# Batch norm with ReLU on one core: the read of `beta` moves from the scalar queue to the gpsimd queue

## The chip, the cores and the metric

The kernel runs on one core of a Trainium2 chip. The metric is the device time in microseconds (us) of one execution. The kernel before took 83.83 us, the median of 4 runs between 83.75 and 84.23 us. A core has five engines, each with its own instruction stream: TensorE (PE), VectorE (DVE), ScalarE (ACT), GpSimd (POOL) and SyncE (SP). Data moves between HBM and on-chip memory by DMA: an engine issues a transfer from its stream (the profile writes SPq, ACTq, POOLq for that), and 16 DMA engines, shared by all queues, carry it out in packets.

## The reference, cut to what matters

The input `x` is [32, 128, 32, 32] in float32, so 16.78 MB; the output has the same size. Four vectors of 128 numbers hold the parameters of each channel.

```python
def reference(x, gamma, beta, running_mean, running_var, eps):
    normalized = (x - running_mean[None, :, None, None]) / np.sqrt(running_var[None, :, None, None] + eps)
    scaled = normalized * gamma[None, :, None, None] + beta[None, :, None, None]
    return np.maximum(scaled, 0).astype(np.float32)
```

Per channel this is one multiply, one add and a ReLU: `relu(x * scale + bias)` with `scale = gamma / sqrt(running_var + eps)` and `bias = beta - running_mean * scale`.

## The kernel before

**Tiling.** Batch and channel are flattened into 4096 rows of 1024 numbers (4 KB). A partition takes J = 16 rows that lie next to each other, so 128 partitions hold 2048 rows, and there are two such halves (t = 0 and 1). `PIECES` cuts each half along the 16 rows: rows 0-2, 2-4, 4-8 and 8-16 of half 0, rows 0-8 and 8-16 of half 1. That makes six load tiles of 1, 1, 2, 4, 4 and 4 MB (in units of 1024 KB). Each has its own buffer, so no load waits for a buffer.

**Loads.** All six are issued on the sync queue (line 52), in that order. Each partition of a tile is one packet, of 8, 8, 16, 32, 32 and 32 KB.

**Parameters.** Because 16 rows are 16 neighbouring channels, a partition needs 16 channels, and partitions 0 to 7 together need all 128; the pattern repeats every 8 partitions. The four vectors are read into the tile `raw`, 8 partitions by 4 by 16, by four transfers of 512 bytes on the scalar queue (line 59), in the order running_var, gamma, running_mean, beta. GpSimd makes a 0/1 matrix `rep` meanwhile (lines 63 and 64), and one matmul (line 74) of `rep` with `raw` spreads the four vectors to 128 partitions (`cols`). The matmul reads the whole of `raw`, so it waits for all four transfers. Then follow a square root on ScalarE (line 82, with a load of its function table before it) and four small operations on VectorE (lines 84 to 90), which end in `scale_t` and `bias_t`.

**Main loop.** ScalarE goes over the tiles in load order; one activation (line 96) does one row of all partitions, 128 x 1024, in place, and at the end of a tile the same queue issues its store (line 104). `STORE_CUTS` has the first tile stored in two parts of 512 KB, so there are seven stores. ScalarE's order is the program's own (`manual_schedule`); on the other engines the framework orders the instructions.

**Semaphores.** Each transfer counts up a semaphore when it has landed. In the trace of the kernel before, the seventeen transfers of the two queues share eight of these in turn. A transfer that takes a semaphore over waits, on the issuing queue, until the one that had it before has landed: the fourth load waits for running_var, the fifth for running_mean, the sixth for the second load.

**End.** After the last store has landed, SyncE checks the semaphores in turn, all engines meet at a barrier, and GpSimd clears the semaphores (line 138).

Of the kernel before, what the change touches and what calls it, by code (L numbers as in the profile page):

```python
# [1 line left out]

# [4 lines left out]


F32 = mybir.dt.float32
ACTF = mybir.ActivationFunctionType  # L10

J = 16

PIECES = (((0, 2), (2, 4), (4, 8), (8, 16)), ((0, 8), (8, 16)))

STORE_CUTS = {(0, 1)}


@with_exitstack
def kernel(
    ctx: ExitStack,
    tc: tile.TileContext,
    x: bass.AP,
    gamma: bass.AP,
    beta: bass.AP,
    running_mean: bass.AP,
    running_var: bass.AP,
    eps: bass.AP,  # L30
    out: bass.AP,
):
    nc = tc.nc
    B, C, H, W = x.shape
    HW = H * W
    P = nc.NUM_PARTITIONS
    assert C % J == 0 and P % (C // J) == 0 and (B * C) % (P * J) == 0
    Q = C // J
    T = B * C // (P * J)

    xr = x.rearrange("b c h w -> (b c) (h w)").rearrange("(t p j) w -> t p j w", p=P, j=J)
    outr = out.rearrange("b c h w -> (b c) (h w)").rearrange("(t p j) w -> t p j w", p=P, j=J)

    data = ctx.enter_context(tc.tile_pool(name="data", bufs=1))
    params = ctx.enter_context(tc.tile_pool(name="params", bufs=1))
    psum = ctx.enter_context(tc.tile_pool(name="psum", bufs=1, space=bass.MemoryType.PSUM))

    tiles = []
    for t in range(T):
        for a, b in PIECES[t]:  # L50
            xt = data.tile([P, b - a, HW], F32, name=f"x{t}_{a}")
            nc.sync.dma_start(out=xt, in_=xr[t, :, a:b, :])  # L52
            tiles.append((t, a, b, xt))

    raw = params.tile([Q, 4, J], F32, name="raw")
    for k, src in enumerate((running_var, gamma, running_mean, beta)):
        nc.scalar.dma_start(out=raw[:, k, :], in_=src.rearrange("(q j) -> q j", j=J))
    eps_t = params.tile([P, 1], F32, name="eps_t")  # L60
    nc.vector.memset(eps_t, float(eps))  # L61
    rep = params.tile([Q, P // Q, Q], F32, name="rep")
    nc.gpsimd.memset(rep, 1.0)  # L63
    nc.gpsimd.affine_select(  # L64
        out=rep,
        in_=rep,
        compare_op=mybir.AluOpType.is_equal,
        fill=0.0,
        base=0,
        pattern=[[0, P // Q], [-1, Q]],  # L70
        channel_multiplier=1,
    )
    cols = psum.tile([P, 4, J], F32, name="cols")
    nc.tensor.matmul(  # L74
        cols.rearrange("p k j -> p (k j)"),
        rep.rearrange("q r s -> q (r s)"),
        raw.rearrange("q k j -> q (k j)"),
        start=True,
        stop=True,
    )  # L80
    std_t = params.tile([P, J], F32, name="std_t")
    nc.scalar.activation(out=std_t, in_=cols[:, 0, :], func=ACTF.Sqrt, bias=eps_t[:, 0:1], scale=1.0)  # L82
    rstd_t = params.tile([P, J], F32, name="rstd_t")
    nc.vector.reciprocal(out=rstd_t, in_=std_t)  # L84
    scale_t = params.tile([P, J], F32, name="scale_t")
    nc.vector.tensor_mul(out=scale_t, in0=cols[:, 1, :], in1=rstd_t)  # L86
    ms_t = params.tile([P, J], F32, name="ms_t")
    nc.vector.tensor_mul(out=ms_t, in0=cols[:, 2, :], in1=scale_t)  # L88
    bias_t = params.tile([P, J], F32, name="bias_t")
    nc.vector.tensor_sub(out=bias_t, in0=cols[:, 3, :], in1=ms_t)  # L90

    with tc.manual_schedule(engines={mybir.EngineType.Activation}):
        for t, a, b, xt in tiles:
            first = a
            for j in range(a, b):
                nc.scalar.activation(  # L96
                    out=xt[:, j - a, :],
                    in_=xt[:, j - a, :],
                    func=ACTF.Relu,
                    bias=bias_t[:, j : j + 1],  # L100
                    scale=scale_t[:, j : j + 1],
                )
                if j + 1 == b or (t, j + 1) in STORE_CUTS:
                    nc.scalar.dma_start(
                        out=outr[t, :, first : j + 1, :], in_=xt[:, first - a : j + 1 - a, :]
                    )
                    first = j + 1


# [1 line left out]
_INS = ['x', 'gamma', 'beta', 'running_mean', 'running_var', 'eps']  # L111
_OUTS = [((32, 128, 32, 32), 'float32')]

_NUMBERS = {'eps': 1e-05}


# [26 lines left out]
```

## Time and profile before

| What | Where from | Value |
|---|---|---|
| Time of the profiled execution | times | 83.75 us |
| Its span, first to last instruction | profile page | 81.9 us |
| Median of the runs | times | 83.83 us |
| ScalarE busy | page, part 1 | 38.5 us (47%) |
| GpSimd busy | page, part 1 | 0.8 us (1%), all of it before 1.5 us |
| HBM traffic | page, part 3 | 16.78 MB read, 16.78 MB written |
| Issue of the four parameter reads on ACT | timeline | 0.59, 0.29, 0.31 and 0.39 us, from 0.81 to 2.48 us |
| Start of the matmul that needs them | timeline | 7.49 us |
| First activation of the main loop | timeline | 9.48 us |
| Last store issued | timeline | 55.93 us |

The span is what the profiler sees of the program's own instructions; 1.85 us of the execution's time lie outside it. The issue of a transfer (an ACTq or SPq line) is only the time in which the engine's queue hands it over. The transfer itself runs afterwards on the DMA engines, and whoever needs the data shows up with a wait "<-DMA ...". Idle time before an instruction stands in square brackets behind it in a timeline, with what ended it.

### The profile page before, as it was taken

The numbers are of one execution on the slowest core, as the hardware profiler recorded it, in microseconds if no ns is written. First come the engines' busy times: TensorE is split into PE (matmuls) and PEld (weight loads), VectorE is DVE, ScalarE is ACT, GpSimd is POOL, SyncE is SP. The second block draws the span as 40 slices with busy tenths as digits, with TensorE's granted clock in tenths as the row PEclk, the third lists the DMA queues.
The fourth block names the chain that finished last, engine by engine and source line by source line (L and its number), as shares of the span: only waits on it lengthen the run. The fifth ranks groups of instructions, "written<-read, shape, count | busy, mean of one in ns | idle before, by whom it ended". The sixth has DMA issues, their size and how long they took to land.

```text
span 81.9 us, 119 instructions
## 1 busy us (share of the span) xinstructions
PE 0.7 (1%) x2; PEld 0.5 (1%) x2; DVE 0.8 (1%) x5; ACT 38.5 (47%) x34; POOL 0.8 (1%) x6
## 2 busy tenths in 40 slices
PE   0003000000000000000000000000000000000000
PEld 0002000000000000000000000000000000000000
DVE  0000300000000000000000000000000000000000
ACT  0600477799039999199994199993000000000000
POOL 3000000000000000000000000000000000000000
DMA  1999998989899999979799798998999799699690
GB/s 36 352 405 481 416 520 352 512 352 496 368 464 400 460 404 460 436 308 588 320 396 564 328 440 384 512 512 352 416 512 432 336 512 480 288 512 496 272 512 0
DMA packets 1936, 33.56 MB, mean 410 GB/s; under 512 B 272, under 2 KB 272, under 8 KB 528
## 3 DMA queue, kind: packets, MB, share of 16 engines
q1 hardware_dynamic: 864, 16.78, 48.4%
q10 hardware_dynamic: 1072, 16.78, 47.8%
HBM read 16.78 MB, written 16.78 MB: 410 GB/s over the span
## 4 chain that ended last, share of the span: by engine, by line
DMA 56%; ACT 11%; SPq 0%; issue 0%
DMA x<-in_x_dram 56%; ACT x L96 11%; SPq L52 0%
## 5 line engine op out<-in xcount | busy, mean ns | idle before, releaser
L96 ACT ACTIVATE x<-x,bias_t,scale_t 128x1024 f32<-128x1024 f32 x32 | 37.0, 1227 | 10.5 <-DMA x<-in_x_dram 8.1
L82 ACT ACT_TABLE_LOAD x1 | 1.3, 1283 | 2.6 <-issue 2.6
L82 ACT ACTIVATE std_t<-cols,eps_t 128x16 f32<-128x16 f32 x1 | 0.3, 274 | 4.3 <-PE cols L74 4.3
L74 PE MATMUL cols<-raw,rep 8*128 8x64 f32 x2 | 0.7, 428 | 7.5 <-DMA raw<-in_beta_dram 7.5
L74 PEld LDWEIGHTS cols<-raw,rep 8*128 8x128 f32 x2 | 0.5, 306 | 7.5 <-issue 7.5
L64 POOL TENSOR_SCALAR_AFFINE_SELECT rep<-rep 8x128 f32<-8x128 f32 x1 | 0.4, 393 | 0.1
L84 DVE RECIPROCAL rstd_t<-std_t 128x16 f32<-128x16 f32 x1 | 0.3, 255 | 7.5 <-ACT std_t L82 7.5
L63 POOL MEMSET rep<- 8x128 f32 x1 | 0.2, 194 | 0.3 <-POOLq L124 0.3
L86 DVE TENSOR_TENSOR scale_t<-cols,rstd_t 128x16 f32<-128x16 f32 x1 | 0.2, 174 | 0.1
L88 DVE TENSOR_TENSOR ms_t<-cols,scale_t 128x16 f32<-128x16 f32 x1 | 0.2, 174 | 0.0
L90 DVE TENSOR_TENSOR bias_t<-cols,ms_t 128x16 f32<-128x16 f32 x1 | 0.2, 174 | 0.0
L124 POOL MEMSET const-bfloat16-1.0<- 128x1 bf16 x1 | 0.1, 108 | 0.0
L124 POOL MEMSET const-uint8-127<- 128x1 uint8 x1 | 0.1, 108 | 0.0
L124 POOL MEMSET const-float32-0.0<- 128x1 f32 x1 | 0.1, 105 | 0.3 <-issue 0.3
L124 POOL MEMSET const-float32-1.0<- 128x1 f32 x1 | 0.1, 105 | 0.0
L61 DVE MEMSET eps_t<- 128x1 f32 x1 | 0.1, 59 | 0.9 <-PEq L124 0.9
## 6 DMA issues: line engine op xcount, KB each, us to landing
x<-in_x_dram SPq DMA_DIRECT2D x3, 4096.0 KB, 38.7
out_dram<-x ACTq DMA_DIRECT2D x3, 4096.0 KB, 28.0
x<-in_x_dram SPq DMA_DIRECT2D x2, 1024.0 KB, 5.7
x<-in_x_dram SPq DMA_DIRECT2D x1, 2048.0 KB, 11.2
out_dram<-x ACTq DMA_DIRECT2D x1, 2048.0 KB
out_dram<-x ACTq DMA_DIRECT2D x2, 512.0 KB, 19.0
out_dram<-x ACTq DMA_DIRECT2D x1, 1024.0 KB
raw<-in_running_var_dram ACTq DMA_DIRECT2D x1, 0.5 KB
```

Of the source, the lines that this page charges most:

```text
L61: nc.vector.memset(eps_t, float(eps))
L63: nc.gpsimd.memset(rep, 1.0)
L64: nc.gpsimd.affine_select(out=rep, in_=rep, compare_op=mybir.AluOpType.is_equal, fill=0.0, base=0, pattern=[[0, P // Q], [-1, Q]], channel ...
L74: nc.tensor.matmul(cols.rearrange("p k j -> p (k j)"), rep.rearrange("q r s -> q (r s)"), raw.rearrange("q k j -> q (k j)"), start=True, s ...
L82: nc.scalar.activation(out=std_t, in_=cols[:, 0, :], func=ACTF.Sqrt, bias=eps_t[:, 0:1], scale=1.0)
L84: nc.vector.reciprocal(out=rstd_t, in_=std_t)
L86: nc.vector.tensor_mul(out=scale_t, in0=cols[:, 1, :], in1=rstd_t)
L88: nc.vector.tensor_mul(out=ms_t, in0=cols[:, 2, :], in1=scale_t)
L90: nc.vector.tensor_sub(out=bias_t, in0=cols[:, 3, :], in1=ms_t)
L96: nc.scalar.activation(out=xt[:, j - a, :], in_=xt[:, j - a, :], func=ACTF.Relu, bias=bias_t[:, j : j + 1], scale=scale_t[:, j : j + 1],)
L124: nc = _bacc.Bacc("TRN2", target_bir_lowering=False, num_devices=1)
```

## The change

The loop over the four vectors chooses the queue by the source: `beta` is issued by gpsimd, the other three by scalar as before. Source, destination and size of each transfer are as before, and so is everything else in the program text.

```diff
     raw = params.tile([Q, 4, J], F32, name="raw")
     for k, src in enumerate((running_var, gamma, running_mean, beta)):
-        nc.scalar.dma_start(out=raw[:, k, :], in_=src.rearrange("(q j) -> q j", j=J))
+        eng = nc.gpsimd if src is beta else nc.scalar
+        eng.dma_start(out=raw[:, k, :], in_=src.rearrange("(q j) -> q j", j=J))
     eps_t = params.tile([P, 1], F32, name="eps_t")
```

## The prediction

> **What bounds the kernel now.** I read the page first, its slices before its groups:
>
> ```profile
> span 81.9 us, 119 instructions
> ...
> DMA  1999998989899999979799798998999799699690
> ...
> q1 hardware_dynamic: 864, 16.78, 48.4%
> q10 hardware_dynamic: 1072, 16.78, 47.8%
> ...
> DMA x<-in_x_dram 56%; ACT x L96 11%; SPq L52 0%
> ```
>
> No engine has a row that is full; the DMA row is at 7 to 9 tenths from the second slice to the second last. Part 3 says the same: packets of the load queue (q1) and the store queue (q10) fill 48.4 + 47.8 = 96.2% of the span on all 16 DMA engines, 78.8 us. Next the stretches of the windows view (start:end and length; then busy us with a count for PE, PEld, DVE, ACT and POOL; last the clock, the DMA share and GB/s):
>
> ```profile
> 0.00:1.80 1.80, 0.00 (x0) 0.00 (x0) 0.06 (x1) 0.00 (x0) 0.80 (x6) 1.00 0.04 9
> 1.80:2.80 1.00, 0.00 (x0) 0.00 (x0) 0.00 (x0) 0.23 (x1) 0.00 (x0) 1.00 0.84 213
> 2.80:46.70 43.90, 0.65 (x2) 0.50 (x2) 0.78 (x4) 29.13 (x26) 0.00 (x0) 1.00 1.01 431
> 46.70:80.60 33.90, 0.00 (x0) 0.00 (x0) 0.00 (x0) 9.16 (x8) 0.00 (x0) 1.00 0.99 425
> 80.60:80.95 0.35, 0.00 (x0) 0.00 (x0) 0.00 (x0) 0.00 (x0) 0.00 (x0) 1.00 0.00 0
> 80.95:81.90 0.95, 0.00 (x0) 0.00 (x0) 0.00 (x0) 0.00 (x0) 0.00 (x0) 1.00 0.00 0
> ```
>
> So the execution is a sum of four stretches: 1.80 us to the first load packet, a ramp of 1.00 us at half rate (213 GB/s; at 431 it would take 0.5 us, so the ramp loses 0.5), 77.8 us with all DMA engines full, and 1.3 us from the last data to the last instruction. With 1.85 us outside the span that is 83.75. The chain's second half, eight activations of the last tile, hides this: it ends at 55.90 and the store behind it lands at 80.93, 25 us later, because older stores stand before it. The limit is the bytes, not the chain.
>
> **The parameter path**, from the timeline:
>
> ```profile
> 0.81 0.59 ACTq L59 DMA_DIRECT2D raw<-in_running_var_dram  x1
> ...
> 1.07 0.39 POOL L64 TENSOR_SCALAR_AFFINE_SELECT rep<-rep 8x128 f32<-8x128 f32 x1
> ...
> 2.09 0.39 ACTq L59 DMA_DIRECT2D raw<-in_beta_dram  x1
> 2.57 1.28 ACT L82 ACT_TABLE_LOAD   x1 [2.57 <-issue]
> 7.49 0.65 PE L74 MATMUL cols<-raw,rep 8*128 8x64 f32 x2 [7.49 <-DMA raw<-in_beta_dram]
> 8.18 0.27 ACT L82 ACTIVATE std_t<-cols,eps_t 128x16 f32<-128x16 f32 x1 [4.32 <-PE cols L74]
> ...
> 9.48 1.24 ACT L96 ACTIVATE x<-x,bias_t,scale_t 128x1024 f32<-128x1024 f32 x1 [1.02 <-DVE bias_t L90]
> ```
>
> The matmul waits for beta, the last of the four. The semaphores in the trace give the landings: running_var 2.19 us, gamma 6.08, running_mean 6.72, beta 7.35. The last three come 0.63 to 0.64 us apart, in order: each is two packets long on a DMA engine (64 bytes of data and the semaphore), and each such packet stands behind one 8 KB load packet of 0.31 us.
>
> **The change, part by part.**
>
> *Removed from ACT:* one issue of 0.39 us. The table load starts at about 2.14 to 2.18 instead of 2.57 and ends near 3.45; ScalarE then waits for the matmul in any case (idle 4.32 us before line 82), so this is worth nothing. If that cover were gone it would be 0.4 us on the start of the main loop.
>
> *Added to POOL:* one transfer issue. The trace has no transfer from POOL, so I bound its landing from both sides. Early: like running_var, 1.38 us from issue (0.81 to 2.19), so near 2.2. Late: like beta itself, 5.26 us from issue (2.09 to 7.35), begun only behind the affine select (end 1.46), so 6.72. The Trainium skill's "DMA: Bandwidth & Descriptors", section "Anatomy of one DMA — SWDGE (gpsimd) path", gives such a transfer about 2.0 us fixed, hence 2.8 by estimate; its first-byte figures (about 1 us against 0.6 for the scalar path, under "Latency and other measured facts") speak against the change, by 0.4 us. The rows weigh more here: beta took 5.26 us, not 2, since it stood between load packets. I take 3 to 6.7 us; in all of it running_mean, at 6.72, becomes the last one. The matmul, square root and first activation then move 7.35 - 6.72 = 0.63 us earlier, the activation to 8.85; the first tile is there since 5.47. If GpSimd issues beta ahead of lines 63 and 64, `rep` moves back by that issue; its reader is the same matmul, and between 1.46 and 7.46 there are 6 us of cover.
>
> *What 0.63 us at the main loop is worth:* nothing. From 2.8 to 46.7 the DMA engines run at 431 GB/s whatever they carry; a store that starts earlier takes its turns from the loads. The last store is issued at 55.93 but could not start its bulk before the one ahead of it lands, at 71.25 (trace); issue to first packet is about 1 us (0.81 to 1.80 for the first load). So the main loop has 71.25 - 1 - 55.93 = 14.3 us to spare.
>
> *Moved:* the shared semaphores. The queue's own waits show what stands there:
>
> ```profile
> SPq L52 <- DMA raw<-in_running_mean_dram: 3.9, 1, 3.9
> SPq L52 <- DMA x<-in_x_dram: 0.9, 1, 0.9
> ```
>
> With beta out of the turn of eight, the fifth load would wait for gamma (6.08) instead of running_mean, the fourth for nothing. At 6.7 us some 6 MB of issued loads still stand in the queue, the fourth lands at 23.77; worth nothing. Worst, a load waits for the first store (25.1): the fifth is in the queue until 34.73 then, still nothing.
>
> *Added to the DMA engines:* 8 data packets stay, in another queue; a few more semaphore packets of 9 ns. Below 0.01 us each. *Added at the end:* one more semaphore to check and clear, at the step of SyncE's last checks: 80.985 to 81.047, 0.06 us.
>
> **Sum:** 83.75 + 0.06 = 83.81 for the profiled execution; the median stands 0.08 above that execution, so 83.89, rounded to **83.9 us**, own range 83.6 to 84.15.
>
> **Rivals.**
>
> 1. *A third queue costs fixed time outside the full stretch* (slower). Its place is the 1.85 us outside the span and the 0.95 us of closing work, where GpSimd drains and clears. The rule that speaks for it is the Trainium skill's "Runtime: NRT & Kernel Launch", section "The ~15µs preamble/postamble breakdown": a reset of the DMA rings belongs to each launch, and the total depends on the DMA setup. Two data queues are used before; if all of the 1.85 us were theirs, a third would add 0.93, the upper end: 83.89 + 0.93 = 84.8. The lower end is nothing. Within the span the nearest row is GpSimd's longest drain, 0.49 us (at 1.04 in the trace) against 0.08 for the one at the end (81.37): +0.41, giving 84.3. It decides from 0.36 us on. Against it: nothing in the trace of before shows a cost per queue. By the row the sum is 83.9 to 84.3, by the rule up to 84.8; I take 84.5 for the case.
> 2. *The ramp fills sooner* (faster). Between 1.80 and 2.80 four small and four large issues of ACT and SP overlap (running_var's took 0.59 us, gamma's 0.29). If thinning them lets the load packets come at full rate, at most the 0.5 us of the ramp goes: 83.4. Against it: beta's issue begins at 2.09, when the first load packets are already on all engines, and these first ones are slow themselves.
> 3. *Beta comes very late* (slower). It costs only from 7.35 + 14.3 = 21.6 us on, one for one; 15 us from issue to landing would still be free. Landing at 23 us would give 85.3. Nothing is near that.
> 4. *The framework orders POOL so that beta's read changes nothing visible:* same time as the forecast, 83.9, and counted with it.
>
> **Numbers.** A measurement of this kernel can tell about 0.5%, 0.42 us, so "same" is 83.41 to 84.25. Forecast with rival 4: 0.48, of which 0.44 the same and 0.02 on each side. Rival 1: 0.34, of which 0.31 slower and 0.03 the same. Rival 2: 0.14, of which 0.12 faster and 0.02 the same. Rival 3: 0.04, slower. Faster 0.14, same 0.49, slower 0.37. The range, 83.35 to 84.8, takes in the ramp's and the third queue's ends; beyond it lie rival 3 and the outer parts of 1 and 2, less than 0.2.
>
> **What would show it.** Right: the matmul released by running_mean near 6.75 us, the first activation near 8.85, the DMA row as full as before, the last store landing near 80.9, the loads ending within 1 us of 46.7. Rival 1: the stretch from the first packet to the last is unchanged and the closing part, or time less span, is longer. Rival 2: over 300 GB/s between 1.8 and 2.8 us. Rival 3: the matmul released by beta after 20 us. Wrong in its base would be a gap in the DMA row, or a full-rate stretch of another length with the same bytes: then the DMA engines' rate itself depends on the queues.

## The result, and the profile after

The changed kernel took 84.02 us, the median of 37 runs between 83.77 and 84.87, against 83.83 us of the kernel before (58 runs, 83.71 to 84.23). The ratio is 1.004, with a 95% interval of 1.0028 to 1.0051: 0.19 us slower, and within the 0.5% that the prediction counted as the same. Two things stand out in the single executions. The time less the span is 2.05 us on average (38 executions with the profiled one, 2.01 to 2.10), where the profiled execution of before had 1.885 (83.75 less 81.865; the 1.85 above comes from the span rounded to 81.9). And 12 of the 37 lie above 84.35 us, 13 of 38 with the profiled one, where none of before lies. Without these late ones the median is 83.99 us, so most of the difference is there without them.

The profiled execution of the changed kernel, 84.84 us, is one of those. Its page, in the lines that answer to those of before (part 2's DMA row, then queues with packets, MB and share of the 16 engines, then the chain by line):

```profile
span 82.8 us, 120 instructions
...
DMA  1999996979797979798898899899979969997960
...
q1 hardware_dynamic: 864, 16.78, 48.0%
q10 hardware_dynamic: 1056, 16.78, 47.2%
q0 software_dynamic: 32, 0.00, 0.0%
...
DMA x<-in_x_dram 56%; ACT x L97 11%; SPq L52 0%
```

A third queue, q0, has come in with 32 small packets; sixteen small packets have left q10. The two large queues take 95.2% of 82.8 us, 78.8 us on all 16 engines, just what they took before (96.2% of 81.9). So the extra 0.9 us of this execution is not more work on average. The stretches of its windows view, in the same columns as before the change:

```profile
1.80:2.80 1.00, 0.00 (x0) 0.00 (x0) 0.00 (x0) 0.64 (x1) 0.77 (x3) 1.00 0.82 180
2.80:46.50 43.70, 0.66 (x2) 0.50 (x2) 0.78 (x4) 28.71 (x26) 0.00 (x0) 1.00 1.01 428
46.50:80.45 33.95, 0.00 (x0) 0.00 (x0) 0.00 (x0) 9.16 (x8) 0.00 (x0) 1.00 1.00 432
80.45:80.75 0.30, 0.00 (x0) 0.00 (x0) 0.00 (x0) 0.00 (x0) 0.00 (x0) 1.00 0.02 0
80.75:81.55 0.80, 0.00 (x0) 0.00 (x0) 0.00 (x0) 0.00 (x0) 0.00 (x0) 1.00 0.00 0
81.55:81.95 0.40, 0.00 (x0) 0.00 (x0) 0.00 (x0) 0.00 (x0) 0.00 (x0) 1.00 0.00 0
81.95:82.80 0.85, 0.00 (x0) 0.00 (x0) 0.00 (x0) 0.00 (x0) 0.00 (x0) 1.00 0.00 0
```

The engines run full until about 80.45, as before until 80.60, and then hardly anything moves for 1.5 us. The trace's packets and semaphores say what is waited for. Fifteen of the sixteen DMA engines report their share of the last store between 80.74 and 81.03 us; the sixteenth does so at 81.89. Most of that delay is one load packet of 32 KB on this engine, which began at 45.45 and took 1.87 us, where such packets take 1.21: 0.66 us of the 0.86 by which the engine is the last at the end. The sixth load lands by 46.84 on all other engines and at 48.00 on this one, but half a microsecond of that is older. The engine had been the last with the fourth and the fifth load as well (24.07 against 23.74, and 35.20 against 34.78), and with the second store the first (35.37 against 35.83 and later), so that part is in the main another order of loads and stores. In the profiled execution of before, the sixteen report the last store between 80.58 and 80.93.

The start, from the timeline of the changed kernel:

```profile
1.32 0.67 POOL L60 DMA_DIRECT2D raw<-in_beta_dram  x1 [0.79 <-POOLq L125]
1.44 0.29 ACTq L60 DMA_DIRECT2D raw<-in_gamma_dram  x1
1.76 0.31 ACTq L60 DMA_DIRECT2D raw<-in_running_mean_dram  x1
...
2.16 1.28 ACT L83 ACT_TABLE_LOAD   x1 [2.16 <-issue]
2.25 0.40 POOL L65 TENSOR_SCALAR_AFFINE_SELECT rep<-rep 8x128 f32<-8x128 f32 x1
...
6.97 0.66 PE L75 MATMUL cols<-raw,rep 8*128 8x64 f32 x2 [6.97 <-DMA raw<-in_running_mean_dram]
...
8.96 1.24 ACT L97 ACTIVATE x<-x,bias_t,scale_t 128x1024 f32<-128x1024 f32 x1 [1.02 <-DVE bias_t L91]
```

GpSimd begins beta's read at 1.32, before the work on `rep`, and beta lands at 6.54, 5.2 us later. The matmul is now released by running_mean (landed at 6.84), 0.52 us earlier than before, and the main loop starts 0.52 us earlier. This execution, with its late engine, can't show what that is worth at the end; the runs below say more.

### The profile page after: what moved, and what is told of

Read it like the earlier page. It is cut to its first block, busy times and chain, and to the rows that moved or that the text cites. A ratio compares the mean times of both kernels' runs of the same rounds, so it can differ in the third digit from the quotient of the medians.

```text
span 82.8 us, 120 instructions
## 1 busy us (share of the span) xinstructions
PE 0.7 (1%) x2; PEld 0.5 (1%) x2; DVE 0.8 (1%) x5; ACT 38.5 (47%) x34; POOL 1.5 (2%) x7
## 4 chain that ended last, share of the span: by engine, by line
DMA 56%; ACT 11%; SPq 0%; issue 0%
DMA x<-in_x_dram 56%; ACT x L97 11%; SPq L52 0%
## 5 line engine op out<-in xcount | busy, mean ns | idle before, releaser
L60 POOL DMA_DIRECT2D raw<-in_beta_dram x1 | 0.7, 669 | 0.8 <-POOLq L125 0.8
```

The source lines that it names most:

```text
L60: eng.dma_start(out=raw[:, k, :], in_=src.rearrange("(q j) -> q j", j=J))
```

## The experiments

Four theories stood against each other:

- **A:** a third queue costs a fixed time outside the span.
- **B:** the gpsimd queue's transfer makes one DMA engine late.
- **C:** the earlier main loop changes how loads and stores collide, and that makes an engine late.
- **D:** the time outside the span follows the length of ScalarE's program, which lost one instruction. A variant, **E**, takes the number of transfers on the scalar queue instead.

D came up with the first four runs; E goes with it. "Outside" below is the mean of time less span over all executions of a run. "Late" counts the executions above 84.35 us. Lengths of ScalarE's program are those of the built program, with its waits and closing instructions; each trace shows two instructions fewer, with the same steps between the runs. Runs a to d, e to h and i to l were taken on three chips, each group beside the kernel before; those are the three sets of numbers in the first row. The chip of the first measurement is not on record.

| Run | ScalarE's program | gpsimd reads | Median us | Ratio to before, interval | Mean span | Outside | Late |
|---|---|---|---|---|---|---|---|
| before (35, 28 and 33 runs) | 58 | 0 | 83.92, 83.84, 83.97 | | 82.05, 82.03, 82.11 | 1.886, 1.885, 1.884 | 0 of 96 |
| first measurement, after | 57 | 1 | 84.02 | 1.004, 1.0028 to 1.0051 | 82.15 | 2.05 | 13 of 38 |
| a_before_twice | 58 | 0 | 84.03 | 1.001, 0.9999 to 1.0021 | 82.14 | 1.886 | 0 of 11 |
| b_after_again | 57 | 1 | 83.99 | 1.0007, 0.9997 to 1.0017 | 81.94 | 2.068 | 0 of 11 |
| c_three_vectors | 57 | 0 | 83.99 | 1.0018, 0.9999 to 1.0037 | 82.06 | 2.057 | 3 of 12 |
| d_extra_gpsimd_read | 58 | 1 | 84.09 | 1.0024, 1.0014 to 1.0034 | 82.23 | 1.888 | 0 of 12 |
| e_after_two_tiny | 58 | 1 | 83.81 | 0.9994, 0.9982 to 1.0007 | 81.97 | 1.880 | 0 of 12 |
| f_before_two_tiny | 59 | 0 | 83.73 | 0.9981, 0.9965 to 0.9997 | 82.08 | 1.706 | 0 of 12 |
| g_after_late_start | 57 | 1 | 84.26 | 1.0037, 1.0022 to 1.0051 | 82.18 | 2.049 | 1 of 11 |
| h_all_four_gpsimd | 52 | 4 | 84.50 | 1.006, 1.004 to 1.008 | 82.70 | 1.735 | 4 of 6 |
| i_after_four_tiny | 60 | 1 | 83.71 | 0.9974, 0.9964 to 0.9985 | 81.94 | 1.795 | 0 of 11 |
| j_before_four_tiny | 61 | 0 | 83.92 | 1.0008, 0.9991 to 1.0025 | 82.05 | 1.918 | 1 of 11 |
| k_after_third | 57 | 1 | 83.98 | 1.0004, 0.9994 to 1.0014 | 81.92 | 2.058 | 0 of 11 |
| l_after_fourth | 57 | 1 | 83.97 | 1.0004, 0.9993 to 1.0015 | 81.93 | 2.067 | 0 of 11 |

### The kernel before, once more

No edit.

> The kernel before, once more, as a measure of what no change looks like. Every theory: ratio 1.000, interval within 0.2%; no execution above 84.3 us; the time less the span near 1.85 us as in the profiled execution of before (83.75 less 81.9).

Ratio 1.001, with 1.000 in the interval only just; the mean span differs by 0.09 us from that of the same kernel beside it. So a single difference of 0.1% or of 0.1 us in the span says nothing here. The time outside is 1.886 us in both.

### The changed kernel, once more

No edit.

> The changed kernel, once more on this chip, with a second trace. If the change makes one DMA engine fall behind, about a third of the executions lie above 84.35 us and the others near 84.0; ratio about 1.003 to 1.005. Theory A (a third queue costs a fixed time outside the span): time less span about 2.05 us in every execution, also in the quick ones. Theory B (the gpsimd queue's transfer makes one DMA engine late): the late engine is seen again as one landing of the last store 0.4 us or more behind the other fifteen in the slower executions. Theory C (it is the moved start of the main loop and of the stores that changes how loads and stores collide, not the queue): no difference to A or B here.

The time outside is there again, 2.07 us. The late executions are not: 11 executions between 83.93 and 84.27. The ratio falls to 1.0007. The second trace has no late engine:

```profile
1.80:2.80 1.00, 0.00 (x0) 0.00 (x0) 0.00 (x0) 0.63 (x1) 0.77 (x3) 1.00 0.94 262
2.80:46.50 43.70, 0.66 (x2) 0.49 (x2) 0.78 (x4) 28.73 (x26) 0.00 (x0) 1.00 1.01 429
46.50:80.30 33.80, 0.00 (x0) 0.00 (x0) 0.00 (x0) 9.16 (x8) 0.00 (x0) 1.00 1.00 431
80.30:80.70 0.40, 0.00 (x0) 0.00 (x0) 0.00 (x0) 0.00 (x0) 0.00 (x0) 1.00 0.02 0
80.70:80.95 0.25, 0.00 (x0) 0.00 (x0) 0.00 (x0) 0.00 (x0) 0.00 (x0) 1.00 0.00 0
80.95:81.90 0.95, 0.00 (x0) 0.00 (x0) 0.00 (x0) 0.00 (x0) 0.00 (x0) 1.00 0.00 0
```

In this windows view the full stretch ends at 80.3 and the program at 81.9. The sixteen DMA engines report the last store between 80.64 and 81.03 us, close to the kernel before (80.58 to 80.93).

### Without beta, and without the gpsimd queue

```diff
-    raw = params.tile([Q, 4, J], F32, name="raw")
-    for k, src in enumerate((running_var, gamma, running_mean, beta)):
+    raw = params.tile([Q, 3, J], F32, name="raw")
+    for k, src in enumerate((running_var, gamma, running_mean)):
...
-    nc.vector.tensor_sub(out=bias_t, in0=cols[:, 3, :], in1=ms_t)
+    nc.vector.tensor_scalar_mul(out=bias_t, in0=ms_t, scalar1=-1.0)
```

> Beta is not read at all (the bias is minus mean times scale; the sum with beta is left out), and the gpsimd queue stays unused. ScalarE issues three reads and the semaphores turn as in the changed kernel. Matmul near 6.8 us, first activation near 8.9 in all theories. Theory C: as the changed kernel, 84.0 and a tail up to 84.8. Theories A and B: as before, 83.83, no execution above 84.3, time less span 1.85.

This refutes A and B as they stood. No transfer runs on the gpsimd queue, and yet the time outside is 2.057 us and 3 of 12 executions lie at 84.49 to 84.63. Neither effect needs the gpsimd queue. For the time outside, taking a read off ScalarE is enough. For the late executions that is not shown: run b, with the same number of reads on ScalarE and on the same chip, had none. The edit leaves beta out of the sum.

### Before, with an additional read on the gpsimd queue

```diff
         nc.scalar.dma_start(out=raw[:, k, :], in_=src.rearrange("(q j) -> q j", j=J))
+    junk = params.tile([Q, J], F32, name="junk")
+    nc.gpsimd.dma_start(out=junk, in_=beta.rearrange("(q j) -> q j", j=J))
```

> The kernel before, with its four reads on the scalar queue, and in addition one read of beta on the gpsimd queue into a tile that nobody reads. The start of the main loop stays at 9.4 to 9.6 us. Theory A: 84.03, time less span 2.05. Theory B: a third of the executions above 84.35. Theory C: 83.83 as before, no tail.

The counterpart: the gpsimd queue runs, and the time outside stays at 1.888 us. No execution is late. The median is 0.17 us above before, all of it in the span (82.23 against 82.05), and the second run of before had half of that difference itself. The additional read stands in its timeline, and the parameter path did not get quicker by it:

```profile
1.32 0.67 POOL L61 DMA_DIRECT2D junk<-in_beta_dram  x1 [0.79 <-POOLq L126]
...
7.87 0.66 PE L76 MATMUL cols<-raw,rep 8*128 8x64 f32 x2 [7.87 <-DMA raw<-in_beta_dram]
...
9.86 1.24 ACT L98 ACTIVATE x<-x,bias_t,scale_t 128x1024 f32<-128x1024 f32 x1 [1.02 <-DVE bias_t L92]
```

The matmul waits for beta on the scalar queue until 7.87, as it did in the kernel before (7.49), and here a little longer.

What the two kernels with 2.06 us have in common, against the two with 1.89, is the scalar queue: one transfer fewer, and one instruction fewer in ScalarE's program. Hence D and E.

### The changed kernel with ScalarE's program at its old length

```diff
     nc.vector.memset(eps_t, float(eps))
+    junk = params.tile([P, 1], F32, name="junk")
+    for _ in range(2):
+        nc.scalar.activation(out=junk, in_=eps_t, func=ACTF.Sqrt)
```

Two are needed for one more instruction, since the first takes over a wait that stood alone.

> The changed kernel, with two square roots of one number per partition added on ScalarE under the cover of its wait for the matmul; with them ScalarE's program has 58 instructions, as in the kernel before, instead of 57. The reads and the start of the main loop stay as in the changed kernel (matmul about 6.97 us). Theory D (time less span is set by the length of ScalarE's program: 1.89 us at 58, 2.06 at 57): 1.89. Theory E (it is set by the number of transfers on the scalar queue, 10 instead of 11): 2.06. Theory C (the earlier main loop makes single DMA engines late): some executions 0.4 us or more above the median; if D is the cause of these too, none.

The time outside goes back to 1.880 us with 10 transfers on the scalar queue, so E falls and D stands. Since c has the same length without the gpsimd queue and d the old length with it, the 0.17 us go with ScalarE's program and not with the queue. The time is 83.81 us against 83.84: with ScalarE's program at its old length the change measures as nothing. No execution is late. Where the additional work goes is seen in the timeline:

```profile
2.09 1.28 ACT L65 ACT_TABLE_LOAD   x1 [2.09 <-issue]
3.38 0.44 ACT L65 ACTIVATE junk<-eps_t 128x1 f32<-128x1 f32 x2
...
7.27 0.66 PE L78 MATMUL cols<-raw,rep 8*128 8x64 f32 x2 [7.27 <-DMA raw<-in_running_mean_dram]
7.96 0.27 ACT L86 ACTIVATE std_t<-cols,eps_t 128x16 f32<-128x16 f32 x1 [4.14 <-PE cols L78]
```

The square roots end at 3.82, and ScalarE still waits 4.14 us for the matmul.

### The kernel before with the same edit

> The kernel before, with the same two square roots; ScalarE's program has 59 instructions, the scalar queue its 11 transfers. Theory D in its simplest form (odd and even lengths): time less span 2.06 us, median 0.17 above before. D as a threshold between 57 and 58: 1.89, median as before. Theory E: 1.89. No theory expects late DMA engines here except one in which the odd length causes them.

Neither form of D: at 59 instructions the time outside falls further, to 1.706 us, and the median to 83.73, although the kernel does more. The reads, the queues and the semaphores are those of before.

### The changed kernel with its main loop put back

```diff
+N_COPIES = 3
...
     nc.vector.tensor_mul(out=ms_t, in0=cols[:, 2, :], in1=scale_t)
+    for _ in range(N_COPIES):
+        nc.vector.tensor_scalar_mul(out=ms_t, in0=ms_t, scalar1=1.0)
```

> The changed kernel with three more multiplications by one on VectorE in the bias's path, which bring the main loop's start back from 8.96 to about 9.6 us. ScalarE's program stays at 57 instructions. Theory D and E: time less span 2.06. Theory C for the late executions: none above 84.4 here, as the stores start where they did before. If they come with the changed kernel's other properties (57 instructions, the turn of the semaphores, fewer reads on the scalar queue): some above 84.4 also here.

2.049 us outside at 57 instructions, as D has it; VectorE's longer program (17 instructions for 14) moves nothing. The highest execution is 84.36, 0.1 us above the median, so none stands apart; but since the changed kernel itself showed none in 33 further executions, this does not confirm C. The median is high, 84.26, because the span is 0.15 above that of before in the mean; the main loop began at 9.75:

```profile
8.92 0.59 DVE L92 TENSOR_SCALAR ms_t<-ms_t 128x16 f32<-128x16 f32 x3
9.54 0.17 DVE L94 TENSOR_TENSOR bias_t<-cols,ms_t 128x16 f32<-128x16 f32 x1
9.75 1.24 ACT L100 ACTIVATE x<-x,bias_t,scale_t 128x1024 f32<-128x1024 f32 x1 [1.65 <-DVE bias_t L94]
```

The run f began at 9.71 and has a mean span of 82.08, so the start alone does not explain 82.18. But, late executions aside, all runs that start about this time have longer spans than those that start near 9.1; the section on the prediction comes back to it.

### All four vectors on the gpsimd queue

```diff
-        eng = nc.gpsimd if src is beta else nc.scalar
+        eng = nc.gpsimd
```

> All four vectors are read by the gpsimd queue; ScalarE's program has 52 instructions, the scalar queue 7 transfers. Theory A by transfer (each gpsimd read costs fixed time): 0.17 us for each, 84.5. Theory D (odd and even): time less span 1.89. E: 2.06 or more. The span itself is bound by the bytes in any theory: 81.9 to 82.2, wherever the main loop starts.

Outside, 1.735 us, below that of before. A by transfer had 0.17 us for each of the four reads, and nothing like it is seen; ScalarE's program is shorter too, so run d remains the plain evidence against it. But the span is 0.67 us longer in the mean, which no theory had. The timeline and the queues:

```profile
1.32 0.67 POOL L60 DMA_DIRECT2D raw<-in_running_var_dram  x1 [0.80 <-POOLq L125]
...
3.00 0.52 POOL L60 DMA_DIRECT2D raw<-in_beta_dram  x1
...
9.90 0.65 PE L75 MATMUL cols<-raw,rep 8*128 8x64 f32 x2 [9.90 <-DMA raw<-in_beta_dram]
...
11.89 1.24 ACT L97 ACTIVATE x<-x,bias_t,scale_t 128x1024 f32<-128x1024 f32 x1 [1.02 <-DVE bias_t L91]
```

```profile
span 82.8 us, 119 instructions
...
q1 hardware_dynamic: 864, 16.78, 48.8%
q10 hardware_dynamic: 1008, 16.78, 47.2%
q0 software_dynamic: 128, 0.00, 0.1%
```

The main loop starts 2.4 us later than before, well inside the 14.3 us of slack, and the store queue does not run dry: the queues still fill 96.1% of the span. But the load queue's packets take 48.8% of 82.8, which is 40.4 us, against 39.6 before, while the store queue's take 39.1 in both. So 0.8 us go to load packets that take longer than their kind, on all engines. In the trace most of that falls between 42 and 46 us: 0.69 us for each engine there, 0.01 in the profiled execution of before. Why they take longer there was not found.

### Longer programs

The edit of e, with four square roots instead of two, on the changed kernel and on the kernel before.

> The changed kernel with four square roots of one number per partition under the cover of ScalarE's wait: 60 instructions in ScalarE's program. So far time less span was 2.05 us at 57, 1.88 at 58 and 1.71 at 59 instructions, and 1.74 at 52. If it falls by 0.17 for each further instruction: 1.53, and 83.5 in all. If it runs in steps of four (52 and 60 alike): 1.74 or lower. If it starts again: 2.05, and 84.0. If the number of transfers set it: 2.05.

> The kernel before with the same four square roots: 61 instructions on ScalarE. Steps of four (57 and 61 alike): time less span 2.05, median 0.17 above before. A fall by 0.17 for each instruction that goes on: 1.36 and 83.3.

1.795 us at 60 and 1.918 at 61 instructions. A steady fall is refuted, and so are steps of four: 60 is 0.06 us above 52 (1.735), and 61 is not 57 (2.05 to 2.07). The time outside depends on the length of ScalarE's program by up to 0.36 us, falls by 0.17 to 0.18 from 57 to 58 and from 58 to 59, and rises again after. Its law stays open, and so does which part of the time outside it is. One trace has a hint: in all traces packets of instruction fetch of 8 KB stand ahead of the span, and in j alone there is also one behind it (at 83.73 us, where the span ends at 81.94). Whether the fetching of instructions makes the difference was not tested.

Run i is also the quickest against both kernels: 83.71 us, ratio 0.9974 (0.9964 to 0.9985) to before, with 0.09 us of it outside and 0.17 in the span, as in k and l below (0.19 and 0.18). No run shows a part of the gpsimd queue in it.

### The changed kernel, twice more

> The changed kernel, for its late executions. If they belong to the change: of these and the next run's executions, some 24, about 8 lie above 84.35. If they belonged to the chip or the hour of the first measurement: none or one, as in the second (none of 11). Time less span 2.05 either way.

> As the run before: the changed kernel loaded once more, so that a property of one loading shows as a difference between these two.

Both ratios are 1.0004, no execution of 22 is late, and the time outside is 2.06 us. With b, that is none of 33 in three runs, against 13 of 38 at first. So the late executions do not come with the change each time; the chip or the loading of the first measurement may have had a part in them. They came in c (3 of 12) as well, and most executions of h lie there with load packets that took longer on all engines; what brings them was not found, and theory C is neither shown nor refuted.

## Why the prediction was right

**The bound.** Bytes on full DMA engines: right. The two queues' packets take 78.8 us before and after, and with beta's read on GpSimd the engines run full over the same stretch.

**ScalarE's issue.** The table load was put at 2.14 to 2.18 and came at 2.16; ScalarE still waits 4.2 us behind it. Worth nothing, as said.

**GpSimd's transfer.** Landing at 6.54, inside the 3 to 6.7 that the rows gave. Of the two ends the late one was near: 5.2 us from issue to landing, as beta took on the scalar queue (5.26). The fixed cost of about 2.0 us from the Trainium skill's "DMA: Bandwidth & Descriptors", section "Anatomy of one DMA — SWDGE (gpsimd) path", does not hold beside load packets here; in run h the four reads took 5.9 to 6.8 us. The transfer began at 1.32, half a microsecond behind the start that I assumed, and ahead of `rep`, which was finished at 2.65 and had its cover.

**The parameter path.** Running_mean as the last one, right; 0.52 us were gained instead of 0.63, with the first activation at 8.96 for 8.85. That they are worth nothing at the end is not what the runs suggest. The ratios of the repeats (1.0004 to 1.0007) hold 0.17 us more outside the span, so the span must be shorter. Leaving out the late executions, the mean span was 81.91 to 81.97 us in every run whose traced main loop began between 8.96 and 9.28 (the first measurement, b, c, e, i, k, l), and 82.02 to 82.23 in every run where it began between 9.48 and 9.86 (before and a, d, f, g, j). Run g, the changed kernel with the start put back, is in the second group, at 82.17; h, at 11.89, has 82.70 over all its executions. So half a microsecond at the start goes with 0.1 to 0.2 us of span. That it is the cause is not shown: each start is that of one execution, the same kernel before began at 9.48 and at 9.68, and only g separates the start from the number of reads on the scalar queue, on another chip than the repeats of the changed kernel.

**"Whatever they carry".** Too strong. Stores that start later or earlier do not starve the engines, but load packets take longer in some executions than in others, 0.6 us for each engine in the profiled execution of before, 1.0 in that of run a, the same kernel, and 1.4 in h. The slack of 14.3 us is right as a bound on starvation and wrong as a promise of no cost.

**The semaphores.** The fifth load waits for gamma, as worked out, and nothing came of it.

**The end.** One more check was priced at +0.06 us. The closing part, from the last landing to the last instruction, went from 0.93 to 0.90 us. The term has the wrong sign and no weight. The last store landed at 81.89 us with the late engine and at 81.03 without it, where the forecast had 80.9.

**Rival 1** had the place right and the cause wrong. Its sign was met: the time outside the span did grow, by 0.17 us of the 0.93 allowed, but a gpsimd read without a shorter ScalarE program leaves it at 1.888 (d), and a shorter ScalarE program without a gpsimd read brings 2.057 (c). The step that was missing is that removing an instruction can itself cost time outside the span. The rule of the Trainium skill's "Runtime: NRT & Kernel Launch", section "The ~15µs preamble/postamble breakdown", that the total depends on the DMA setup, was not seen at work: with a third queue and ScalarE's length as before, run d has 1.888 against 1.886. **Rival 2** and **rival 3** did not happen: 180 and 262 GB/s in the ramp in the two traces of the changed kernel against 213 before, and beta landed in time.

The forecast of 83.9 us stands on the right bound, 78.8 us of packets before and after. That it was met to 0.1 us is in part luck. Two terms of about the same size were missing from the sum and nearly cancel: 0.17 us more outside the span, in every run of the changed kernel, and 0.1 to 0.2 us less in the span in the three repeats. Late executions, a third of the first measurement, were not in it either.

## What to carry to other kernels

Where the DMA row is full from end to end, a shorter start is worth little, here at most 0.1 to 0.2 us of 0.5; look at what the bytes cost, not at who asks for 512 of them. Before a difference of 0.2 us is put down to an edit, split it into span and time outside, run the unchanged kernel against itself, and restore the length of each engine's program. A tail of late executions in one run is not yet a property of the kernel.

## What the runs showed of the hardware that was not expected

- The time outside the span moves with the number of instructions in ScalarE's program: 1.735 us at 52, 2.05 to 2.07 at 57, 1.88 to 1.89 at 58, 1.706 at 59, 1.795 at 60, 1.918 at 61. Two square roots added in idle time made the kernel before 0.1 us quicker (ratio 0.9981, 0.9965 to 0.9997).
- A read of 512 bytes on the gpsimd queue takes as long as one on the scalar queue while loads fill the DMA engines: beta took 5.2 us there, and 5.26 on the scalar queue in the kernel before.
- One load packet of 32 KB took 0.66 us more than its kind (1.87 us against 1.21). The other engines did not take over packets of the engine that was held up: it was 0.85 us behind them at 52 us and 0.86 at the end, which waited for it.
